# Level scores in two column tiles, four samples' outputs at once, the gate's second product stacked, samples' rows transposed once: one decoder layer on one Trainium2 core

## The chip, the cores and the metric

The kernel runs on one core of a Trainium2 chip. The metric is the device time of one execution in microseconds (us). The core has five engines with queues of their own: PE (TensorE: matrix products, with PEld for the loads of their stationary operand), DVE (VectorE), ACT (ScalarE), POOL (GpSimd) and SP (SyncE, which here only issues DMAs).

## The reference

One inference step of a decoder layer for a new sequence of 512 positions and 8 samples with one new token each; the model's width is 2048. All is float32.

```python
def mixer(xn, ...):
    proj = xn @ w_in
    bg, cg, hin, q, k, v, og, glr = jnp.split(proj, [...])
    cu, conv_new = causal_dwconv(cg * hin, conv_prev, conv_w)
    ya = bg * cu
    logf = jax.nn.log_sigmoid((glr @ gate_w2 + gate_b).astype(f32)) / GATE_TAU
    ...
    o, s_new = gla_chunked(qh, kh, vh, lf, gla_prev.astype(f32), chunk)
    ...
    out = jnp.concatenate([ya, yb], axis=-1) @ w_out
```

```python
def trunk(x, ...):
    m, c_new, s_new = mixer(rmsnorm(x, norm_mix_g[l]), ...)
    x = x + m
    f, f_new = conv_ffn(rmsnorm(x, norm_ffn_g[l]), ...)
    x = x + f
    return rmsnorm(x, final_norm_g), ...
```

The gated linear attention (GLA) has 4 heads with keys of 128 and values of 256 columns. Per position S = diag(a) S + k^T v and o = q S; a comes from the gate, glr @ gate_w2, with a rank of 16. For the new sequence S starts at zero, for each of the 8 samples from its state of 128 x 256 in HBM, and the new states are outputs too. The mixer is followed by an output projection and a feed-forward block of width 5632.

## The kernel before, in words

Activations stand with the model's columns on the partitions and the positions in the free dimension: 512 of the sequence and 8 of the samples make 520 columns, worked on as two halves of 260. Each large product is split into high and low parts (hi, lo) for accuracy: for one block of 128 rows (k) there are three products, hi by hi, hi by lo and lo by hi, for each half of the columns. The weights come as pieces of 128 x 1024 by DMA from SP (raw, L101); ACT makes hi (L111), DVE lo (L112). The products of the mixer's input projection are those of L140, those of the later stages L1247 and L1490.

The start (0 to 55 us): x is loaded with positions on the partitions. For each of the 16 column blocks, x_copy transposes four blocks of 128 x 128 (L378) and the samples' 8 x 128 (L379) into one PSUM bank; ACT (the first four blocks, L383) or DVE (L385) copies all 520 columns to SBUF, POOL sends them to HBM for later (L389), and ACT and DVE split them into hi and lo (L126, L127, and L393, L395 for the first two blocks). The first head's q and k products, twelve a block, run between the transposes. The low rank product glr for all heads (L306) follows, and DVE multiplies its first 32 rows, the products with hi and lo of the weights, by the rows' norm (L532).

The heads (55 to about 420 us): product groups of 16 blocks x 6 products fill PE. After each 4 blocks (24 products), a tick, the generator gla_head puts in one step of a head that is ahead in the data:

- the gate's second product w2s by glr (L879), whose 32 rows hold the rank of 16 twice. ACT and DVE form the log of the gate from it (L883 to L889), and DVE sums it along the positions (L892);
- the diagonal scores of k and q (L930), four products of 128 columns, copied under a mask by DVE into the matrix at (L934);
- seven levels, s = 64, 32, ..., 1. For each, POOL makes differences of the summed gate (e), ACT the exponential (L918), DVE two half-products with q and k into L (L919, L922), and PE multiplies the four chunks of L, 128 columns as weights and the 64 columns of the second halves as data (L982). DVE copies the result under a mask into at (L987). L is made two levels ahead;
- the samples, in four pairs: SP loads a pair's states s0 (L942, three buffers) and v rows vb (L946); ACT scales vb (L952), DVE forms the new state (L955), SP stores it (L959). PE multiplies each by its row of q (L968) into rows 32 j of a PSUM bank, j being the sample's number modulo 4. The state is made at the first four levels, and the product goes behind the third to the sixth level, one pair each;
- transposes of the key matrix (L1033), the samples' selection (L1038), then the outputs (L1053, L1058) and the state of the sequence (L1067, L1071).

In this stage a scheduler with priorities sets the order in which each engine gets these instructions; engines take them in that order, and what cannot start blocks all that is behind it. SP's queue holds the weight pieces, the states' loads and the stores. A weight piece's load waits for DVE to have used the buffer's former content.

A float32 product appears in the profile as two records, one of the split kind (fp32r in a tile's type) as one.

Of the kernel before, what the change touches and what calls it, by code (L numbers as in the profile page):

```python
# [17 lines left out]
P = 128  # L18
D = 2048
KD = D // P  # L20
NP = 512
NS = 8
T = NP + NS
HT = T // 2
NH = 4
DV = 256
# [11 lines left out]
def trunk_kernel(  # L38
# [53 lines left out]
    def tmp():  # L92
        return tp.tile([P, T], F32, tag="t", name="t")
# [37 lines left out]
    def halves(t):  # L131
        return t[:, :HT], t[:, HT:T]
# [52 lines left out]
    idn = cp.tile([P, P], F32, name="idn")  # L185
# [49 lines left out]
    glr = cp.tile([P, T], F32, tag="glr", name="glr")[:32, :]  # L235
    gmix, gffn, gb, gng, cw = (
        par[:, 0:16], par[:, 16:32], par[:, 32:36], par[:, 36:44], par[:, 44:68]
    )
# [20 lines left out]
    masks = {}  # L259
# [23 lines left out]
    with ExitStack() as es:  # L283
# [10 lines left out]
        def low_rank_weights():  # L294
            raw = sp.tile([P, KD, RANK], F32, name="wgraw")
            nc.sync.dma_start(raw, w_in[:, 6144:6160].rearrange("(k p) c -> p k c", p=P))
            nc.scalar.activation(wg[:, :, 0:16], raw, AF.Copy)
# [12 lines left out]

        prow = sp.tile([68, P], F32, name="prow")
        xs = sp.tile([NS, D], F32, name="xs")

        xc = [[sp.tile([P, 4, P], F32, name=f"x0{j}") for j in range(4)]]
        xc += [sp.tile([P, 4, 512], F32, name=f"xc{c}") for c in range(1, 4)]
# [23 lines left out]
        nc.scalar.dma_start(prow[0:16, :], norm_mix_g[0].rearrange("(k p) -> k p", p=P))  # L339
        load_x(xc[0][0], 0)  # L340
        nc.scalar.dma_start(xs, x_sample)
        nc.scalar.preload_act_table_set("natural_log_exp_and_others")
        raws = [load_w(0)]
        for j in (1, 2, 3):
# [30 lines left out]
        def x_copy(k):  # L375
            ps = tps()
            for t in range(4):
                nc.tensor.transpose(ps[:, t * P : (t + 1) * P], x_part(k, t), idn)  # L378
            nc.tensor.transpose(ps[:, NP:T], xs[:, k * P : (k + 1) * P], idn[:NS, :NS])  # L379
            st = tmp()[:, :T]  # L380
            copies[k] = st, ps
            if k < 4:
                nc.scalar.activation(st, ps[:, :T], AF.Copy)  # L383
            else:
                nc.vector.tensor_copy(st, ps[:, :T])  # L385

        def x_split(k):
            st, ps = copies.pop(k)
# [139 lines left out]
        )  # L528
        nc.vector.tensor_copy(R, ps[:, :T])
        low_rank_gate(glr_ps, 8, 8)  # L530
        for o, ps, r in zip(halves(glr), glr_ps, halves(R)):
            nc.vector.tensor_tensor(o, ps[:32, :HT], r[:32, :], op=ALU.mult)  # L532
        state_columns()
        make_masks(sp)
        in_order()
# [3 lines left out]
    def bank():  # L539
        return msp.tile([P, 512], F32, tag="ms", name="ms")  # L540
# [246 lines left out]
    with ExitStack() as mix:  # L787
# [44 lines left out]
        with ExitStack() as gl:  # L832
# [9 lines left out]
            for j in range(4):  # L842
# [4 lines left out]
            w2s = gp.tile([32, 512], F32, name="w2s")  # L847
            for i in range(2):
                nc.sync.dma_start(w2s[16 * i : 16 * (i + 1), :], gate_w2[0])

            done = [0]

# [19 lines left out]
            def gla_head(h, q, k, vt):  # L872
# [3 lines left out]
                for b in range(2):  # L876
                    ps = bank()
                    u = slice(b * HT, (b + 1) * HT)
                    nc.tensor.matmul(  # L879
                        ps[:, :HT], w2s[:, h * P : (h + 1) * P], glr[:, u],  # L880
                        start=True, stop=True,
                    )
# [43 lines left out]

                def scores(lhs, rhs, mask):
                    pb = bank()
                    for c in range(4):
                        nc.tensor.matmul(  # L930
                            pb[:, c * P : (c + 1) * P], lhs[:, c, :], rhs[:, c, :],
                            start=True, stop=True,
                        )
                    nc.vector.copy_predicated(  # L934
                        at, mask[:, None, :].to_broadcast([P, 4, P]),
                        pb.rearrange("p (c i) -> p c i", c=4),
                    )


                def sample_load(b0):  # L940
# [20 lines left out]
                    )  # L961
                    return s0

                def sample_out(b0, s0):
                    for i in range(2):
                        b = b0 + i
                        j = b % 4
                        nc.tensor.matmul(  # L968
                            pos[32 * j : 32 * (j + 1), :DV], qm[:, b, :], s0[:, i, :],
                            start=b < 4, stop=b >= 4, tile_position=(0, 32 * j),  # L970
                        )

                def level_scores(L, s):

                    nb = P // (2 * s)
# [3 lines left out]
                    pb = bank()  # L979
                    rhs = second(L)  # L980
                    for c in range(4):
                        nc.tensor.matmul(  # L982
                            pb[:, c * 64 : (c + 1) * 64], L[:, c, :], rhs[:, c],
                            start=True, stop=True,
                        )
                    mask = masks[s].rearrange("p (n h s) -> p n h s", n=nb, h=2)[:, :, 1, :]
                    nc.vector.copy_predicated(  # L987
                        second(at), mask[:, None].to_broadcast([P, 4, nb, s]),
                        pb[:, :256].rearrange("p (c n s) -> p c n s", c=4, n=nb),
                    )  # L990

                scores(k4, q4, idn8)
                Ls = [level(LEVELS[0])]
# [3 lines left out]
                yield  # L997
                yield
                pos = bank()
                s0 = deque()  # L1000
# [95 lines left out]
            for h in range(NH):  # L1096
# [8 lines left out]
                for o, p, rr in zip(halves(q), ps, halves(R)):  # L1105
                    nc.vector.scalar_tensor_tensor(
                        o, p[:, :HT], QSCALE, rr, op0=ALU.mult, op1=ALU.mult
                    )
                vt = gp.tile([P, 4, DV], F32, tag="vt", name="vt", bufs=2)
                v = []  # L1110
# [173 lines left out]
            if t >= 2:  # L1284
                nc.vector.tensor_tensor(z2, z2, R[:, HT:], op=ALU.mult)

    R2 = cp.tile([P, T], F32, tag="glr", name="R2")
    conv_z = {}

    def mult(out, x, y):  # L1290
# [408 lines left out]
    for i, (kind, at, r) in enumerate(order):  # L1699
# [24 lines left out]
        if j == 0:  # L1724
            if n and groups[n - 1][0] in ("mix", "up"):
                before, (t,) = groups[n - 1]
                steps.append([(gate if before == "up" else mix_gate)(t), i, 0])
            if kind == "wo" and at[0] == 1:
                homes.update(FFN_HOMES)
                if not ssq:  # L1730
                    ssq += [cp.tile([P, T], F32, tag="glr", name="ssq"), R]
# [211 lines left out]
```

## Time and profile before

| | us |
|---|---|
| median of 3 runs | 2163.0 |
| lowest, highest | 2161.82, 2163.73 |
| the profiled execution | 2160.99 |
| its span in the trace | 2159.3 |
| PE busy | 2134.2 |
| DVE busy | 1734.5 |
| ACT busy | 1111.6 |
| POOL busy | 439.7 |

The clock granted to PE was 0.997 of full speed. In a row of the profile stand the line of the kernel, the engine, the operation, the output's and inputs' names (buffer numbers left out: ms is any of the small PSUM banks, mm one of the accumulators, tp a bank of the start), the shapes and the number of instructions. In a timeline the first two numbers are the start and the length of a group of like instructions that follow one another, and the bracket at the end is the idle time before, with what ended it. L numbers are lines of the kernel before.

### The profile page before, as it was taken

What the parts mean: (1) busy time and instruction counts of PE and PEld (TensorE: products, weight loads), DVE (VectorE), ACT (ScalarE), POOL (GpSimd) and SP (SyncE); (2) the same over time, 40 slices, a digit from 0 to 9 for tenths busy, and PEclk for the clock granted to TensorE, in tenths of its full rate; (3) what the DMA queues carried; (4) which work ended last, traced back from release to release, by engine and by line L of the source; (5) the groups of instructions that cost most, each with busy time, mean ns of one, the idle gap of its engine ahead of it and who ended that gap; (6) DMA issues with size and microseconds to landing.
All of it is one profiled execution on the core that took longest, in us unless ns stands there. A gap on an engine that the chain in (4) does not pass through costs nothing.

```text
span 2159.3 us, 43820 instructions
## 1 busy us (share of the span) xinstructions
PE 2134.2 (99%) x17749; PEld 2112.2 (98%) x17749; DVE 1734.5 (80%) x2302; ACT 1111.6 (51%) x1631; POOL 439.7 (20%) x625
## 2 busy tenths in 40 slices
PE   9999999999999999999999999999999999999997
PEld 8999999999999999999999999999999999999997
DVE  7347465588888898998998998998998778888886
ACT  6435435355544586555555555555555554444445
POOL 5113131211243421121221131122121300200000
PEclk9999999999999999999999999999999999999999
DMA  8545464388888996667676676676677866994734
GB/s 258 145 131 157 121 190 121 93 247 215 206 259 248 297 268 181 181 183 189 166 191 176 167 195 179 163 198 178 169 193 192 287 206 161 274 291 134 225 108 158
DMA packets 467163, 415.51 MB, mean 192 GB/s; under 512 B 21641, under 2 KB 426393, under 8 KB 466817
## 3 DMA queue, kind: packets, MB, share of 16 engines
q1 hardware_dynamic: 424081, 289.71, 47.0%
q0 software_dynamic: 42832, 122.93, 21.7%
q8 instruction: 139, 2.28, 0.4%
q14 instruction: 63, 0.52, 0.1%
q10 hardware_dynamic: 48, 0.07, 0.0%
HBM read 299.45 MB, written 80.31 MB: 176 GB/s over the span
## 4 chain that ended last, share of the span: by engine, by line
PE 90%; DMA 3%; DVE 3%; ACT 1%; issue 1%; POOL 0%; SPq 0%; ACTq 0%; DVEq 0%; POOLq 0%
PE mm L1247 34%; PE mm L140 14%; PE ms L1247 14%; PE x L1490 9%; PE y L1490 9%; PE f L1490 3%; PE e L1490 3%; PE ms L982 1%; DMA form<-g_d 1%; DMA g_d<-t 1%; DMA yl<-t_d 0%; DMA yl<-mt_d 0%; PE ms L1836 0%; DMA raw<-raw 0%; PE ms L968 0%
## 5 line engine op out<-in xcount | busy, mean ns | idle before, releaser
L1247 PE MATMUL mm<-yl,hi 128*128 128x260 f32 x1696 | 476.6, 281 | 3.4 <-DVE yl L124 3.4
L1247 PE MATMUL mm<-yh,hi 128*128 128x260 f32 x1696 | 476.1, 281 | 2.4 <-ACT ms L1257 1.2
L1247 PE MATMUL mm<-yh,lo 128*128 128x260 f32 x1696 | 475.2, 280 | 0.8 <-DVE lo L1227 0.8
L1223 ACT ACTIVATE hi<-raw 128x1024 fp32r<-128x1024 f32 x324 | 342.0, 1056 | 233.8 <-issue 89.4
L1227 DVE TENSOR_TENSOR lo<-raw,hi 128x1024 fp32r<-128x1024 f32 x324 | 395.4, 1220 | 36.0 <-ACT hi L1223 33.0
L1227 DVE TENSOR_TENSOR lo<-s,hi 128x1024 fp32r<-128x1024 f32 x243 | 298.4, 1228 | 124.9 <-ACT hi L1223 124.9
L1223 ACT ACTIVATE hi<-s 128x1024 fp32r<-128x1024 f32 x243 | 257.4, 1059 | 220.7 <-PE ms L1247 93.6
L1247 PEld LDWEIGHTS mm<-yl,hi 128*128 128x128 f32 x1696 | 319.8, 189 | 4.0 <-DVE yl L124 4.0
L1247 PEld LDWEIGHTS mm<-yh,hi 128*128 128x128 f32 x1696 | 319.5, 188 | 3.0 <-ACT ms L1257 1.4
L1247 PEld LDWEIGHTS mm<-yh,lo 128*128 128x128 f32 x1696 | 319.2, 188 | 1.2 <-DVE lo L1227 1.2
L1247 PE MATMUL ms<-b,hi 128*128 128x260 f32 x1408 | 266.3, 280 | 0.0
L1247 PEld LDWEIGHTS ms<-b,hi 128*128 128x128 f32 x1408 | 223.2, 189 | 0.0
L1490 PE MATMUL x<-form,hi 128*128 128x260 f32 x1120 | 211.5, 281 | 0.1
L1490 PE MATMUL y<-form,hi 128*128 128x260 f32 x1120 | 211.3, 281 | 0.0
L1168 DVE TENSOR_TENSOR s<-s,raw 128x1024 f32<-128x1024 f32 x162 | 197.9, 1221 | 2.8
L1247 PE MATMUL ms<-b,lo 128*128 128x260 f32 x704 | 198.1, 281 | 0.0
L1490 PEld LDWEIGHTS x<-form,hi 128*128 128x128 f32 x1120 | 176.4, 188 | 0.7 <-issue 0.5
L1490 PEld LDWEIGHTS y<-form,hi 128*128 128x128 f32 x1120 | 176.4, 188 | 0.3
L112 DVE TENSOR_TENSOR lo<-raw,hi 128x1024 fp32r<-128x1024 f32 x76 | 94.9, 1253 | 78.0 <-ACT hi L111 77.9
L1490 PE MATMUL x<-form,lo 128*128 128x260 f32 x560 | 156.7, 280 | 0.1
L1490 PE MATMUL y<-form,lo 128*128 128x260 f32 x560 | 156.7, 280 | 0.0
L1247 PEld LDWEIGHTS ms<-b,lo 128*128 128x128 f32 x704 | 132.4, 188 | 0.0
(382 smaller groups left out, 5066.2 us busy)
## 6 DMA issues: line engine op xcount, KB each, us to landing
raw<-in_w_up_dram SPq DMA_DIRECT2D x176, 512.0 KB, 4.6
raw<-in_w_down_dram SPq DMA_DIRECT2D x96, 512.0 KB, 4.7
raw<-in_w_in_dram SPq DMA_DIRECT2D x92, 512.0 KB, 4.5
form<-f_d SPq DMA_DIRECT2D x126, 260.0 KB, 6.2
raw<-raw POOLq DMA_DIRECT2D x56, 512.0 KB, 5.9
f_d<-t POOLq DMA_DIRECT2D x80, 260.0 KB, 5.6
raw<-in_w_out_dram SPq DMA_DIRECT2D x32, 512.0 KB, 13.8
form<-g_d POOLq DMA_DIRECT2D x42, 260.0 KB, 7.6
```

The costliest lines, as they stand in the source:

```text
L112: nc.vector.tensor_tensor(lo, raw, hi.bitcast(F32), op=ALU.subtract)
L140: nc.tensor.matmul(o, w, xx, start=first and i == 0, stop=last and i == 2)
L982: nc.tensor.matmul(pb[:, c * 64 : (c + 1) * 64], L[:, c, :], rhs[:, c], start=True, stop=True,)
L1168: return lambda: nc.vector.tensor_tensor(out, x, y, op=ALU.add)
L1223: nc.scalar.activation(his[i], src, AF.Copy)
L1227: nc.vector.tensor_tensor(los[i], src, his[i].bitcast(F32), op=ALU.subtract)
L1247: nc.tensor.matmul(st["bank"][b], w[:, k, :], x, start=b not in st["used"] and k == 0 and j == 0, stop=k == 7 and j == 2, skip_group_check ...
L1490: nc.tensor.matmul(ps[:, m, :], w[:, k, m * P : (m + 1) * P], x, start=b not in st["used"] and k == 0 and j == 0, stop=k == 3 and j == 2, ...
```

## The change

Four parts of the heads and of the start are computed in another arrangement.

1. Levels and diagonal scores. The 128 weight columns of a chunk are cut into two tiles of 64, at columns 0 and 64 of PE. A level's product takes from each half only the data columns that belong to it (32 instead of 64), so there are eight products where there were four, and two masked copies on DVE, each over 64 partitions, where there was one. The widest level, s = 64, needs one tile and a plain copy. (L953, L1002, L1017; the copies L958, L1006, L1024.)
2. Samples' outputs. Four samples' products go together, behind the third level (samples 0 to 3) and the fifth (4 to 7), each on its own tile of 32 columns (L990).
3. The gate's second product. glr and w2s get 96 rows: high by high, high by low and low by high in one stacked product of the split kind (L900). For that ACT makes three copies of the gate's weights at the start and POOL two; glr is copied by ACT, and multiplied and split in head 0 by DVE and ACT; w2s is loaded six times and split.
4. Samples' rows of x. For 14 of the 16 column blocks the transpose of 8 rows (L379 before) goes; one transpose of 128 x 128 of the samples' rows, laid out anew by a DMA, takes their place, and POOL puts each block's 8 columns beside the sequence's 512, which ACT and DVE copy alone.

The scheduler's order changes with it. PE in head 1 before, at the sixth level (its L is L_2441); s0_2406 is the states of pair 3, mm the accumulators of the product group:

```order
L140 MATMUL mm_2461<-bl_97,hi_2465 128x260
L140 MATMUL mm_2462<-cl_99,hi_2465 128x260
L982 MATMUL ms_2547<-L_2441 128x64 [waits DVE_49,PE_49]
L982 MATMUL ms_2547<-L_2441 128x64 x3
L968 MATMUL ms_2293<-s0_2406,qm_848 32x256 [waits DMAHW7_49,DVE_49]
L968 MATMUL ms_2293<-s0_2406,qm_848 32x256 [waits DVE_49]
L140 MATMUL mm_2461<-xh_100,hi_2471 128x260 [waits Activation_49]
```

The same pair in PE's order now; its state is s0_2478, and s0_2423 is pair 2:

```order
L140 MATMUL mm_2536<-bl_89,hi_2540 128x260
L140 MATMUL mm_2537<-cl_91,hi_2540 128x260
L1017 MATMUL ms_2574<-L_2463 64x32 [waits DVE_49,PE_49]
L1017 MATMUL ms_2574<-L_2463 64x32 x7
L990 MATMUL ms_2353<-s0_2423,qm_858 32x256 [waits DMAHW2_49]
L990 MATMUL ms_2353<-s0_2423,qm_858 32x256
L990 MATMUL ms_2353<-s0_2478,qm_858 32x256 [waits DMAHW4_49,DVE_49]
L990 MATMUL ms_2353<-s0_2478,qm_858 32x256 [waits DVE_49]
L140 MATMUL mm_2536<-bh_92,hi_2540 128x260
```

Pair 3's products have moved from behind the sixth level to behind the fifth, into one step with pair 2's.

SP in head 1 before, around the load of pair 3's states (s0_2406); raw are weight pieces, s0_3144 is a load for the next head:

```order
L946 DMA vb_2408<-v_d_123 128x512 [waits DMAHW3_49]
L101 DMA raw_2638<-in_w_in_dram 128x8x128 [waits DMAHW4_49,DVE_49]
L959 DMA out_6_dram<-s0_2358 128x2x256 [waits DMAHW5_49,DVE_49]
L101 DMA raw_2784<-in_w_in_dram 128x8x128 [waits DMAHW6_49,DVE_49]
L942 DMA s0_2406<-in_state_gla_dram 128x2x256 [waits DMAHW7_49,DMAHW0_49,PE_49]
L942 DMA s0_3144<-in_state_gla_dram 128x2x256 [waits DMAHW2_49,PE_49]
```

And now, with pair 3's states in s0_2478:

```order
L970 DMA vb_2480<-v_d_123 128x512 [waits DMAHW0_49]
L101 DMA raw_2728<-in_w_in_dram 128x8x128 [waits DMAHW1_49,DVE_49]
L101 DMA raw_2874<-in_w_in_dram 128x8x128 [waits DMAHW3_49,DMAHW2_49,DVE_49]
L983 DMA out_6_dram<-s0_2423 128x2x256 [waits DVE_49]
L966 DMA s0_2478<-in_state_gla_dram 128x2x256 [waits DMAHW5_49,DMAHW4_49,PE_49]
L966 DMA s0_3239<-in_state_gla_dram 128x2x256 [waits DMAHW6_49,PE_49]
```

The load of pair 3's states still stands behind two weight pieces; the store of pair 2's states has moved behind the second piece.

The diff, cut to its core:

```diff
+            for i in range(3):
+                nc.scalar.activation(wg[:, :, 32 * i : 32 * i + 16], raw, AF.Copy)
...
+            for i in (1, 2):
+                nc.gpsimd.tensor_copy(
+                    wg[:, :, 32 * i + 16 : 32 * i + 32], wg[:, :, 16:32].bitcast(F32)
+                )
...
-            nc.tensor.transpose(ps[:, NP:T], xs[:, k * P : (k + 1) * P], idn[:NS, :NS])
+            if k < 2:
+                nc.tensor.transpose(ps[:, NP:T], xs[:, k * P : (k + 1) * P], idn[:NS, :NS])
...
+            if k == 2:
+                nc.tensor.transpose(ps[:, NP : NP + P], xsr, idn)
+                nc.vector.tensor_copy(xsT.rearrange("p k b -> p (k b)"), ps[:, NP : NP + P])
+            if k >= 2:
+                nc.gpsimd.tensor_copy(st[:, NP:], xsT[:, k, :])
...
-                        ps[:, :HT], w2s[:, h * P : (h + 1) * P], glr[:, u],
+                        ps[:, :HT], w2s[:, h * P : (h + 1) * P], glr[:96, u],
...
-                def sample_out(b0, s0):
-                    for i in range(2):
-                        b = b0 + i
-                        j = b % 4
+                def sample_out(b0):
+                    for j in range(4):
                         nc.tensor.matmul(
-                            pos[32 * j : 32 * (j + 1), :DV], qm[:, b, :], s0[:, i, :],
-                            start=b < 4, stop=b >= 4, tile_position=(0, 32 * j),
+                            pos[32 * j : 32 * (j + 1), :DV], qm[:, b0 + j, :],
+                            s0[j // 2][:, j % 2, :],
+                            start=b0 == 0, stop=b0 == 4, tile_position=(0, 32 * j),
                         )
...
-                        nc.tensor.matmul(
-                            pb[:, c * 64 : (c + 1) * 64], L[:, c, :], rhs[:, c],
-                            start=True, stop=True,
+                        for t in tiles:
+                            nc.tensor.matmul(
+                                pb[t, c * 32 : (c + 1) * 32], L[:, c, t],
+                                second(L[:, c : c + 1, t])[:, 0],
+                                start=True, stop=True, tile_position=(0, t.start),
+                            )
+                    for t in tiles:
...
+                    if i in (2, 4):
+                        sample_out(2 * i - 4)
                     if i < 4:
                         s0.append(sample_pair(2 * i, *loaded))
-                    if 2 <= i < 6:
-                        sample_out(2 * i - 4, s0.popleft())
...
+                if h == 0:
+                    nc.vector.tensor_tensor(gate_rows, gate_rows, R[:96, :], op=ALU.mult)
+                    nc.scalar.activation(glr[:96, :], gate_rows, AF.Copy)
+                    nc.vector.tensor_tensor(
+                        glr[64:96, :], gate_rows[64:96, :], glr[64:96, :].bitcast(F32),
+                        op=ALU.subtract,
+                    )
```

More of the change, by code (lines that the diff above doesn't have):

```diff
@@ L234, in trunk_kernel @@
     R = cp.tile([P, T], F32, name="R")
-    glr = cp.tile([P, T], F32, tag="glr", name="glr")[:32, :]
+    glr = cp.tile([P, T + 3], F32R, tag="glr", name="glr")[:, 3:]
     gmix, gffn, gb, gng, cw = (
@@ L378, in x_copy @@
                 nc.tensor.transpose(ps[:, t * P : (t + 1) * P], x_part(k, t), idn)
-            nc.tensor.transpose(ps[:, NP:T], xs[:, k * P : (k + 1) * P], idn[:NS, :NS])
+            n = T if k < 2 else NP
+            if k < 2:
+                nc.tensor.transpose(ps[:, NP:T], xs[:, k * P : (k + 1) * P], idn[:NS, :NS])
             st = tmp()[:, :T]
             copies[k] = st, ps
+            if k == 2:
[3 more added lines that the diff above has]
+                nc.gpsimd.tensor_copy(st[:, NP:], xsT[:, k, :])
             if k < 4:
-                nc.scalar.activation(st, ps[:, :T], AF.Copy)
+                nc.scalar.activation(st[:, :n], ps[:, :n], AF.Copy)
             else:
-                nc.vector.tensor_copy(st, ps[:, :T])
+                nc.vector.tensor_copy(st[:, :n], ps[:, :n])
         def x_split(k):
@@ L530, in trunk_kernel @@
         low_rank_gate(glr_ps, 8, 8)
-        for o, ps, r in zip(halves(glr), glr_ps, halves(R)):
-            nc.vector.tensor_tensor(o, ps[:32, :HT], r[:32, :], op=ALU.mult)
+        gate_rows = tmp()[:96, :T]
+        for o, ps in zip(halves(gate_rows), glr_ps):
+            nc.scalar.activation(o, ps[:96, :HT], AF.Copy)
         state_columns()
@@ L846, in trunk_kernel @@
                 )
-            w2s = gp.tile([32, 512], F32, name="w2s")
-            for i in range(2):
-                nc.sync.dma_start(w2s[16 * i : 16 * (i + 1), :], gate_w2[0])
+            w2raw = wp.tile([P, 1024], F32, tag="raw", name="raw")[:96, :512]
+            for i in range(6):
+                nc.sync.dma_start(w2raw[16 * i : 16 * (i + 1), :], gate_w2[0])
+            w2s = gp.tile([96, 512], F32R, name="w2s")
+            nc.scalar.activation(w2s, w2raw, AF.Copy)
+            nc.vector.tensor_tensor(
+                w2s[32:64, :], w2raw[32:64, :], w2s[32:64, :].bitcast(F32), op=ALU.subtract
+            )
             done = [0]
@@ L928, in scores @@
                     pb = bank()
+                    tiles = [slice(t, t + 64) for t in (0, 64)]
                     for c in range(4):
-                        nc.tensor.matmul(
-                            pb[:, c * P : (c + 1) * P], lhs[:, c, :], rhs[:, c, :],
-                            start=True, stop=True,
-                        )
[L934 to L937, printed above, removed]
+                        for t in tiles:
+                            nc.tensor.matmul(
+                                pb[t, c * 64 : (c + 1) * 64], lhs[:, c, t], rhs[:, c, t],
+                                start=True, stop=True, tile_position=(0, t.start),
+                            )
+                    for t in tiles:
+                        nc.vector.copy_predicated(
+                            at[t, :, t], mask[t, None, t].to_broadcast([64, 4, 64]),
+                            pb[t, :256].rearrange("p (c i) -> p c i", c=4),
+                        )
                 def sample_load(b0):
@@ L962, in sample_pair @@
                     return s0
-                def sample_out(b0, s0):
-                    for i in range(2):
-                        b = b0 + i
-                        j = b % 4
+                def sample_out(b0):
+                    for j in range(4):
                         nc.tensor.matmul(
-                            pos[32 * j : 32 * (j + 1), :DV], qm[:, b, :], s0[:, i, :],
-                            start=b < 4, stop=b >= 4, tile_position=(0, 32 * j),
+                            pos[32 * j : 32 * (j + 1), :DV], qm[:, b0 + j, :],
+                            s0[j // 2][:, j % 2, :],
+                            start=b0 == 0, stop=b0 == 4, tile_position=(0, 32 * j),
                         )
+                    s0.clear()
                 def level_scores(L, s):
-                    nb = P // (2 * s)
+                    pb = bank()
+                    if s == 64:
+                        for c in range(4):
+                            nc.tensor.matmul(
+                                pb[:64, c * 64 : (c + 1) * 64], L[:, c, :64], L[:, c, 64:],
+                                start=True, stop=True,
+                            )
+                        nc.vector.tensor_copy(
+                            at[:64, :, 64:], pb[:64, :256].rearrange("p (c i) -> p c i", c=4)
+                        )
+                        return
+                    nb = 32 // s
                     second = lambda x: x.rearrange(
@@ L978, in level_scores @@
                     )[:, :, :, 1, :]
-                    pb = bank()
-                    rhs = second(L)
+                    tiles = [slice(t, t + 64) for t in (0, 64)]
                     for c in range(4):
-                        nc.tensor.matmul(
-                            pb[:, c * 64 : (c + 1) * 64], L[:, c, :], rhs[:, c],
-                            start=True, stop=True,
-                        )
[L986 to L990, printed above, removed]
+                        for t in tiles:
+                            nc.tensor.matmul(
+                                pb[t, c * 32 : (c + 1) * 32], L[:, c, t],
+                                second(L[:, c : c + 1, t])[:, 0],
+                                start=True, stop=True, tile_position=(0, t.start),
+                            )
+                    for t in tiles:
+                        mask = masks[s][t, t].rearrange("p (n h s) -> p n h s", n=nb, h=2)
+                        nc.vector.copy_predicated(
+                            second(at[t, :, t]),
+                            mask[:, None, :, 1, :].to_broadcast([64, 4, nb, s]),
+                            pb[t, :128].rearrange("p (c n s) -> p c n s", c=4, n=nb),
+                        )
                 scores(k4, q4, idn8)
@@ L1285, in up_finish @@
                 nc.vector.tensor_tensor(z2, z2, R[:, HT:], op=ALU.mult)
-    R2 = cp.tile([P, T], F32, tag="glr", name="R2")
+    R2 = cp.tile([P, T + 3], F32, tag="glr", name="R2")[:, 3:]
     conv_z = {}
@@ L1730, in trunk_kernel @@
                 if not ssq:
-                    ssq += [cp.tile([P, T], F32, tag="glr", name="ssq"), R]
+                    ssq += [cp.tile([P, T + 3], F32, tag="glr", name="ssq")[:, 3:], R]
                 steps.append([projected(at[1]), i, 0])
```

8 lines of the change are left out of this document (6 added, 2 removed).

## The prediction

> **What bounds the kernel now.** I read the page's busy shares first, then the table of windows over the stages that the change touches, then PE's timeline there.
>
> ```profile
> span 2159.3 us, 43820 instructions
> ...
> PE 2134.2 (99%) x17749; PEld 2112.2 (98%) x17749; DVE 1734.5 (80%) x2302; ACT 1111.6 (51%) x1631; POOL 439.7 (20%) x625
> ```
> ```profile
> 12.80:22.00 9.20, 9.19 (x70) 8.16 (x69) 6.23 (x12) 5.20 (x11) 2.17 (x4) 1.00 1.09 366
> 22.00:31.00 9.00, 9.00 (x71) 8.25 (x70) 7.10 (x13) 7.28 (x18) 3.22 (x5) 1.00 0.98 328
> 31.00:42.00 11.00, 10.39 (x80) 9.44 (x79) 10.93 (x12) 7.81 (x14) 6.40 (x9) 1.00 0.89 246
> ...
> 170.00:255.00 85.00, 83.16 (x672) 79.44 (x671) 52.47 (x88) 36.23 (x57) 19.21 (x24) 1.00 0.46 137
> ```
>
> PE is busy in all but 25 us of the span. Behind each stretch and its length stand the busy times of PE, PEld, DVE, ACT and POOL. Work taken off PE moves the end, but only where nothing else is nearly as late. Two places are in doubt: DVE at the start (10.93 of 11.00 us in the third row), and the attention heads, where PE already idles for 1.84 us in head 1 (the last row). The profiled execution took 2160.99 us, 2.0 under the median of 2163.0; the sum is made against the former and the difference carried to the latter.
>
> **The change part by part: what it takes off PE.** First the levels, in PE's timeline of head 0.
>
> ```profile
> 101.38 0.40 PE L140 MATMUL mm<-xl,hi 128*128 128x260 f32 x2
> 101.62 1.00 PE L982 MATMUL ms<-L 128*128 128x64 f32 x8
> 102.42 0.48 PE L140 MATMUL mm<-xh,hi 128*128 128x260 f32 x2
> 102.74 0.40 PE L140 MATMUL mm<-xh,lo 128*128 128x260 f32 x2
> ```
>
> Two products of 260 columns take 0.24 us (101.38 to 101.62). The level holds PE for 0.80, and the pair behind it takes 0.32 instead of 0.24: 0.88 in all. Its eight records follow every 0.10 us though each streams a quarter of the columns of a product that needs 0.12, so what paces them is the 128-column weight load of each. After the change there are 16 records, in eight pairs on the two halves of the columns, each with a load of 64 columns. Whether the halves work at the same time is shown by the samples' outputs, which already lie on column tiles, of 32 (PE, then PEld).
>
> ```profile
> 109.14 1.00 PE L982 MATMUL ms<-L 128*128 128x64 f32 x8
> 110.07 0.63 PE L968 MATMUL ms<-s,qm 128*32 128x256 f32 x4
> 110.62 0.39 PE L140 MATMUL mm<-bh,hi 128*128 128x260 f32 x1
> 110.85 0.28 PE L140 MATMUL mm<-ch,hi 128*128 128x260 f32 x1
> ```
> ```profile
> 110.06 0.14 PEld L968 LDWEIGHTS ms<-s,qm 128*32 128x32 f32 x4
> ```
>
> Four records of 0.39 us each fill only 0.63, and four loads only 0.14: the two tiles run side by side, in two steps that start 0.24 apart. Level and pair take 1.48 up to the next product, which is late by another 0.11 (0.23 instead of 0.12): 1.59, of it 0.71 for the pair, 0.48 for its two steps and 0.23 for going into the tiles and out again. So a level in two tiles takes 8 steps of 0.05 (a load half as wide) to 0.10 (no faster) and 0.23: 0.63 to 1.03. I take 0.74, near the low end because the 32-column loads were short. 24 levels (all but the widest, 4 heads) give 24 x 0.14 = 3.4 us (from -3.6 to +6); the diagonal scores and the widest level, with as many loads, 8 x 0.13 = 1.0. [...]
>
> Four samples at once are again two steps, 0.48 and part of the 0.23, since PE comes from column tiles already: 0.6 instead of 1.42, 8 x 0.82 = 6.6 us (1.8 if the four tiles take turns in pairs). Next the gate's second product.
>
> ```profile
> 88.09 1.14 PE L879 MATMUL ms<-glr,w2s 32*128 32x260 f32 x4
> 89.16 0.50 PE L140 MATMUL mm<-xh,hi 128*128 128x260 f32 x2
> 89.50 0.40 PE L140 MATMUL mm<-xh,lo 128*128 128x260 f32 x2
> ```
>
> It takes 1.07, the pair behind it is late by 0.10, and it started 0.09 late: 1.26. Two products of 260 columns of the ordinary kind take its place: 0.24. Four heads save 4.1 us. GLA in all: 3.4 + 1.0 + 6.6 + 4.1 = 15.1.
>
> At the start, four transposes and the samples' small one stand against four plain ones, whose price is shown by those of v in head 0:
>
> ```profile
> 31.64 0.60 PE L378 MATMUL tp<-idn,xc 128*128 128x128 f32 x4
> 32.33 0.50 PE L140 MATMUL mm<-xh,hi 128*128 128x260 f32 x2
> 32.67 0.40 PE L140 MATMUL mm<-xh,lo 128*128 128x260 f32 x2
> ```
> ```profile
> 69.70 0.60 PE L856 MATMUL ms<-idn,v 128*128 128x128 f32 x4
> 70.06 0.36 PE L140 MATMUL mm<-bh,hi 128*128 128x260 f32 x1
> 70.27 0.28 PE L140 MATMUL mm<-ch,hi 128*128 128x260 f32 x1
> ```
>
> 0.69 + 0.10 against 0.36 + 0.09: the small one costs 0.34. Fourteen go, one of 128 columns comes (0.1): 4.7 us. The whole sum for PE is 19.8 us.
>
> **What takes it back.** Pair 3, samples 6 and 7, is the large item. Its product stood behind the sixth level; now it goes with pair 2 behind the fifth (s = 4), one tick of 24 products earlier. PE's rows give where the outputs behind the fifth level start in the four heads, DVE's where the pair's two updated states (L955) are made; SP's show the load that they wait for.
>
> ```profile
> 118.99 0.63 PE L968 MATMUL ms<-s,qm 128*32 128x256 f32 x4
> ...
> 202.53 0.63 PE L968 MATMUL ms<-s,qm 128*32 128x256 f32 x4
> ...
> 286.22 0.63 PE L968 MATMUL ms<-s,qm 128*32 128x256 f32 x4
> ...
> 385.92 0.63 PE L968 MATMUL ms<-s,qm 128*32 128x256 f32 x4
> ```
> ```profile
> 118.10 0.88 DVE L955 SCALAR_TENSOR_TENSOR s<-s,asm,vb 128x256 f32<-128x256 f32 x2 [3.67 <-issue]
> ...
> 205.12 1.95 DVE L955 SCALAR_TENSOR_TENSOR s<-s,asm,vb 128x256 f32<-128x256 f32 x2 [1.95 <-DMA s<-in_state_gla_dram]
> ...
> 287.94 0.48 DVE L955 SCALAR_TENSOR_TENSOR s<-s,asm,vb 128x256 f32<-128x256 f32 x1
> ...
> 386.43 0.51 DVE L955 SCALAR_TENSOR_TENSOR s<-s,asm,vb 128x256 f32<-128x256 f32 x1
> ```
> ```profile
> 200.25 0.37 SPq L101 DMA_DIRECT2D raw<-in_w_in_dram  x1
> 200.72 1.03 SPq L942 DMA_DIRECT2D s<-in_state_gla_dram  x2
> ```
>
> The states are ready at 118.98, 207.07, 288.42 and 386.94. PE would come to these outputs earlier by 1.02 (gate) + 0.13 + 0.13 (scores, widest level) + 4 x 0.14 (four levels) + 0.82 (first four samples) = 2.66 us. Were the states no earlier, PE would wait 2.65, 7.20, 4.86 and 3.68: 18.4 us, more than the 15.1 saved. They will be somewhat earlier: the load stands in SP's queue behind a weight piece that waits for DVE, whose work follows a chain that the gate's product starts. The gate and the scores give that chain 1.15 us; if it all went with PE it would gain 2.66 and no wait would be new. I take 1.4, near the low end, as the wait is for a DMA (4.4 us from 200.72 to 205.12) and for queues that PE does not drive: 5.6 us in four heads. Queued behind the waiting product are PE's own products, so the wait is paid in full.
>
> The levels' own inputs also bind:
>
> ```profile
> PE ms L982 <- DVE L L922: 1.3, 3, 0.7
> ```
> ```profile
> 200.14 0.44 DVE L987 COPY_PREDICATED at<-mask,ms 128x256 f32<-128x256 uint8 x1
> ```
>
> Three levels find PE waiting already, two of them in head 1, where the gate's saving of 1.0 us will mostly turn into more of it; and each level adds a second masked copy on DVE (two of half the width for the one of 0.44, 0.0 to 0.4 more each). I take 1.3 for head 1 and 0.4 for each other head, 2.5 us (0 to 5). PE held there is not held at pair 3 again: its wait is 18.4 - 5.6 - 2.5 = 10.3. GLA keeps 15.1 - 2.5 - 10.3 = 2.3 us; with a chain gain of 1.15 it keeps 1.3, with 2.66 it keeps 7.
>
> At the start DVE is idle for 2.97 + 1.90 + 0.07 = 4.9 us in the three windows, so 4.7 us less on PE would use it up entirely. POOL gets fourteen small copies and two copies of the gate's weights, and DVE pays while POOL works:
>
> ```profile
> 34.35 2.44 DVE L112 TENSOR_TENSOR lo<-raw,hi 128x1024 fp32r<-128x1024 f32 x1
> ```
> ```profile
> L112 DVE TENSOR_TENSOR lo<-raw,hi 128x1024 fp32r<-128x1024 f32 x76 | 94.9, 1253 | 78.0 <-ACT hi L111 77.9
> ```
>
> Busy time and the mean in ns are the two numbers behind the bar: 2.44 us here against 1.25 as a rule. Each column block's split now also waits for POOL's copy, with the next products behind it. I take half, 2.5 us (1 to 4.7). Two more copies on ACT, the input rows' extra load, and in head 0 a multiply, a copy and two subtractions lie in stretches where ACT or DVE is idle for over a quarter of the time; that idle time covers them (some 3 us of engine time without it).
>
> Sum: 2.3 + 2.5 = 4.8 us saved, 2156.2 for the profiled execution, 2158 against the median. By the terms' ends it lies between 2151 (7 + 4.7) and 2161 (1.3 + 1).
>
> **The rivals.** (a) Nothing takes it back: pair 3 moves with PE, DVE keeps up at the start. 19.8 us saved, 2143. For it speaks that all of PE's sums are from rows; against it the DMA wait at 205.12.
>
> (b) The column tiles' loads do not overlap anything, so the tiled levels and scores pay 16 steps: 0.8 to 1.6, so 1.2. Levels lose 24 x 0.32 = 7.7 instead of gaining 3.4, scores lose about 1.3. But PE then comes to pair 3 later by some 2.3 us a head, and most of that wait goes, as does part of the wait for levels. In GLA 15.1 - 11.1 - 1.8 = 2.2 is left, less 1.1 and some 1.4 of waits, with 2.5 at the start: about 2161, no difference that can be told.
>
> (c) Slower: pair 3's states land late. A load of the same queue in head 1 has taken far longer than 4.4 us:
>
> ```profile
> 187.84 0.47 SPq L946 DMA_DIRECT2D vb<-v_d  x1
> ```
> ```profile
> 194.98 0.51 ACT L952 ACTIVATE vb<-vb,k 128x256 f32<-128x256 f32 x1 [2.17 <-DMA vb<-v_d]
> ```
>
> That is 7.1 us. If PE runs ahead and the weights' loads crowd the state's load to that, each head waits 2.7 us more: +11, so 2169. From 1.2 us later a head (landing after 5.6 us) the gain is gone.
>
> **How the numbers follow.** This kernel's measurement can tell about 0.2%, 4.3 us, from no change: faster means under 2158.7, slower over 2167.3. The forecast has 0.55, of it 0.40 faster, 0.13 same, 0.02 slower, since its centre lies at the edge and the chain's gain was taken low. (a) has 0.10, all faster. (b) has 0.12: 0.03, 0.08, 0.01. (c) has 0.18: 0.03 same, 0.15 slower. 0.05 is for what I do not see, shared by same and slower (0.03, 0.02). Together: faster 0.53, same 0.27, slower 0.20. The range leaves out most of (a) and the far end of (c): 2145 to 2168.
>
> **What would show it.** Right: L990 behind the fifth level waits for DVE's state update or its load in each head, by 1.5 to 4 us; levels near 0.74; gate 0.24; k blocks of the start under 2.0 us apart but with DVE full. Wrong: levels over 0.9 (b), no wait at L990 (a), waits over 5 us (c), or PE waiting elsewhere in the heads.

## The result and the profile after

The changed kernel's median is 2164.67 us against 2162.3 us before (22 runs each; one of the changed kernel's took 7107.61 us and is left out of the ratio); the ratio is 1.0014, with a 95% interval of 1.0007 to 1.002. It is slower by 2.4 us, less than the 0.2% that was to count, but on the other side of the forecast of 2158. The profiled execution took 2167.36 us, 2.7 more than the median, so single sums of its trace are some us too large; before's took 2160.99, 1.3 under its median.

The page and the windows of the heads (PE, PEld, DVE, ACT, POOL busy, then the granted clock):

```profile
PE 2128.5 (98%) x17952; PEld 2104.0 (97%) x17952; DVE 1748.6 (81%) x2332; ACT 1112.7 (51%) x1637; POOL 447.8 (21%) x641
```
```profile
88.00:170.00 82.00, 80.51 (x721) 76.61 (x720) 40.79 (x74) 38.55 (x65) 18.07 (x23) 0.98 0.55 157
170.00:255.00 85.00, 79.48 (x695) 74.72 (x694) 52.65 (x93) 35.56 (x56) 19.66 (x24) 0.96 0.44 127
255.00:355.00 100.00, 96.57 (x866) 92.83 (x866) 60.23 (x105) 46.13 (x76) 26.14 (x32) 1.00 0.55 159
355.00:420.00 65.00, 62.24 (x569) 58.14 (x568) 43.62 (x77) 25.59 (x42) 17.24 (x20) 0.97 0.39 113
```

PE is busy for 5.7 us less than before, and the end is later. In head 1's window it idles for 5.5 us instead of 1.84, and in three of the windows the granted clock falls under 1.00. PE's waits up to 460 us, summed by what ended them, of after:

```profile
PE ms L990 <- DVE s L979: 7.2, 8, 1.8
PE ms L1017 <- DVE L L943: 3.2, 4, 1.4
PE mm L140 <- DVE lo L112: 1.1, 2, 0.6
...
PE ms L1002 <- DVE L L943: 0.9, 1, 0.9
```

L990 are the samples' outputs, L979 the states that they need. The outputs were not among PE's waits before, nor were those for the weights' low parts (L112). The prices of the instructions are nearly those forecast: a level is 16 records in 0.6 us, the four samples follow in 0.57 where two pairs took 1.42, and the gate's product stands in the stream for 0.24.

```profile
108.16 0.66 PE L1017 MATMUL ms<-L 128*64 128x32 f32 x16
108.74 0.64 PE L990 MATMUL ms<-s,qm 128*32 128x256 f32 x8
109.31 0.39 PE L140 MATMUL mm<-bh,hi 128*128 128x260 f32 x1
```
```profile
88.25 0.40 PE L900 MATMUL ms<-glr,w2s 96*128 96x260 f32 x2
88.49 0.41 PE L140 MATMUL mm<-xh,hi 128*128 128x260 f32 x2
```

From a level's start to the next product it takes 1.15 us with four samples' outputs behind it, when nothing is waited for (behind the third level of head 0). The same place behind the fifth level of head 1:

```profile
201.23 0.66 PE L1017 MATMUL ms<-L 128*64 128x32 f32 x16
201.82 0.63 PE L990 MATMUL ms<-s,qm 128*32 128x256 f32 x4
204.26 0.62 PE L990 MATMUL ms<-s,qm 128*32 128x256 f32 x2 [1.82 <-DVE s L979]
205.70 1.06 PE L990 MATMUL ms<-s,qm 128*32 128x256 f32 x2 [0.82 <-DVE s L979]
206.69 0.59 PE L140 MATMUL mm<-bh,hi 128*128 128x260 f32 x1
207.07 0.42 PE L140 MATMUL mm<-ch,hi 128*128 128x260 f32 x1
207.29 0.42 PE L140 MATMUL mm<-bh,lo 128*128 128x260 f32 x1
```

The first pair of outputs runs at once, the two of the other pair come one by one as DVE makes the states, and the next product starts 5.46 us behind the level, 4.3 late. In heads 0, 2 and 3 the same stretch takes 4.15, 3.89 and 4.34: 13.2 us too much in the four. Of these the list above counts the 7.2 in which PE is idle; the rest is the outputs' own time, as they come one by one, and a slow clock in the last of them (1.06 us here instead of 0.62; the clock granted from 205.7 to 206.7 us was 0.50). The last two rows show a second price: products come every 0.22 us instead of 0.12, at a granted clock of 0.50 (206.7 to 211.6 us). That lasts for 5 us here; the 24 products up to the next level take 4.30, 5.30, 3.06 and 4.02 us in the four heads, 4.4 us more than four times head 2's.

### The profile page after: what moved, and what is told of

Same layout as the page of the kernel before. It is cut to its first block, busy times and chain, and to the rows that moved or that the text cites. A ratio compares the mean times of both kernels' runs of the same rounds, so it can differ in the third digit from the quotient of the medians.

```text
span 2165.6 us, 44293 instructions
## 1 busy us (share of the span) xinstructions
PE 2128.5 (98%) x17952; PEld 2104.0 (97%) x17952; DVE 1748.6 (81%) x2332; ACT 1112.7 (51%) x1637; POOL 447.8 (21%) x641
## 4 chain that ended last, share of the span: by engine, by line
PE 85%; DVE 7%; DMA 3%; issue 2%; ACT 2%; POOL 1%; SPq 0%; DVEq 0%; ACTq 0%; POOLq 0%
PE mm L1292 34%; PE ms L1292 14%; PE mm L140 13%; PE x L1535 8%; PE y L1535 8%; PE e L1535 3%; PE f L1535 3%; DVE lo L1272 1%; DMA raw<-in_w_out_dram 1%; DVE lo L112 1%; DVE s L979 1%; DMA yl<-mt_d 1%; DMA x_d<-acc 1%; DVE yl L124 0%; PE ms L1881 0%
## 5 line engine op out<-in xcount | busy, mean ns | idle before, releaser
L1268 ACT ACTIVATE hi<-raw 128x1024 fp32r<-128x1024 f32 x324 | 341.8, 1055 | 233.6 <-issue 88.2
L112 DVE TENSOR_TENSOR lo<-raw,hi 128x1024 fp32r<-128x1024 f32 x76 | 95.6, 1261 | 72.4 <-ACT hi L111 72.2
L111 ACT ACTIVATE hi<-raw 128x1024 fp32r<-128x1024 f32 x76 | 79.6, 1052 | 106.5 <-PE mm L140 100.7
## 6 DMA issues: line engine op xcount, KB each, us to landing
raw<-in_w_out_dram SPq DMA_DIRECT2D x32, 512.0 KB, 10.3
```

The lines of the kernel that those rows point to most:

```text
L111: nc.scalar.activation(hi, raw, AF.Copy)
L112: nc.vector.tensor_tensor(lo, raw, hi.bitcast(F32), op=ALU.subtract)
L1268: nc.scalar.activation(his[i], src, AF.Copy)
```

## The experiments

Theory A: PE waits behind the fifth level for the states of pair 3, and pays a slow clock on top. Rival B: the levels' inputs or DVE's second masked copies are as late, so that moving the outputs would not help. All times are medians, and ratios are against the kernel before.

**The outputs of samples 4 to 7 one level later.**

```diff
-                    if i in (2, 4):
-                        sample_out(2 * i - 4)
+                    if i in (2, 5):
+                        sample_out(4 * (i == 5))
```

> The changed kernel with the outputs of samples 4 to 7 one level later, behind the sixth (s = 2) instead of the fifth. Theory A (PE waits at these outputs for the states of pairs 2 and 3, some 16 us in the four heads of the changed kernel's trace, and the slow clock behind the waits costs another 5): the place is 24 products and a level, 3.65 us, later, so at most 0.9 us of wait a head is left, no slow stretch, and the kernel takes 2145 to 2152 us, 0.6 to 0.9% under the kernel before. Rival B (the levels' inputs, or DVE with its second masked copy, are as late as the states): PE then waits at the sixth or seventh level instead, and the time stays within 5 us of the changed kernel.

Measured: 2150.52 us, ratio 0.9946 (0.9934 to 0.9959), 11.9 us faster than before and, by the medians, 14.2 faster than the changed kernel. The place in head 1, of this kernel:

```profile
200.33 0.66 PE L1017 MATMUL ms<-L 128*64 128x32 f32 x16
200.92 0.64 PE L990 MATMUL ms<-s,qm 128*32 128x256 f32 x8
201.49 0.50 PE L140 MATMUL mm<-xh,hi 128*128 128x260 f32 x2
```

The eight records run together, and the next product follows 1.16 us behind the level. L990 is gone from the list of waits. What is left there, of the heads:

```profile
PE ms L1017 <- DVE L L943: 2.7, 4, 1.4
PE mm L140 <- DVE lo L112: 1.1, 2, 0.6
PE ms L1002 <- DVE L L943: 0.9, 1, 0.9
```

The windows of the heads show the clock at 1.00 again, and 82.11 us of PE in head 1's 85:

```profile
88.00:170.00 82.00, 82.00 (x762) 78.84 (x762) 45.49 (x83) 42.08 (x70) 19.15 (x24) 1.00 0.55 156
170.00:255.00 85.00, 82.11 (x755) 78.59 (x752) 54.18 (x96) 38.93 (x62) 19.38 (x24) 1.00 0.52 152
```

Of theory A the wait holds, and B does not; what the slow clock costs by itself this run does not separate. This version beats both kernels.

**Two levels later.** The same edit with `i in (2, 6)`.

> The changed kernel with the outputs of samples 4 to 7 two levels later, behind the seventh (s = 1). Theory A: no wait for states is left, so it takes as long as the variant behind the sixth level or up to 3 us less. Against it: the states' buffers are held longer, so the next head's loads start later, and ACT's copy of the outputs comes later; if that matters PE waits at the next head's first outputs and the time is above the other variant's.

Measured: 2152.37 us, 0.9956 (0.9943 to 0.9968). No wait for states either, and not faster than behind the sixth level, where the waits were gone already. The medians differ by 1.9 us the other way, within intervals that overlap.

**The wait filled with work.**

```diff
                 def sample_out(b0):
+                    if b0:
+                        fill = bank()
+                        for _ in range(12):
+                            nc.tensor.matmul(fill[:, :P], ones, ones, start=True, stop=True)
```

> The changed kernel with twelve products of ones ahead of the outputs of samples 4 to 7 in each head, some 3.1 us of PE work that nothing needs, put where PE waits anyway. Theory A with the slow clock as a cost of its own: PE never idles for long, the stretches with products every 0.22 us behind the outputs go, and the kernel is 3 to 5 us faster than the changed one although PE does 12 us more work (2160 to 2163). If the slow stretches cost nothing, or come from something else than the idle time: the same as the changed kernel or up to 2 us slower.

Measured: 2165.06 us, 1.001 (1.0001 to 1.0019), as long as the changed kernel. Head 1 of this kernel (L992 are the products of ones, L994 the outputs):

```profile
199.17 0.66 PE L1021 MATMUL ms<-L 128*64 128x32 f32 x16
199.76 2.94 PE L992 MATMUL ms<-ones 128*128 128x128 f32 x24
202.63 0.64 PE L994 MATMUL ms<-s,qm 128*32 128x256 f32 x8
203.20 0.38 PE L140 MATMUL mm<-bh,hi 128*128 128x260 f32 x1
203.42 0.28 PE L140 MATMUL mm<-ch,hi 128*128 128x260 f32 x1
203.54 0.28 PE L140 MATMUL mm<-bh,lo 128*128 128x260 f32 x1
```

As expected the wait and the slow products behind it are gone (a granted clock of 1.00 in all four windows of the heads), and 2.87 us of useless work a head, 11.5 us, fit in their place. The time did not fall by the 3 to 5 us expected; it is what was expected if the slow stretches cost nothing. The trace is less simple. From the first gate product to the end of the heads this profiled execution takes 369.0 us, the changed kernel's 375.1, and that of the version behind the sixth level 357.4. So in the heads the filling gains 6.1 us, and the wait and the slow clock cost 17.7, near 13.2 + 4.4. Behind the heads the filled kernel loses 3.3 us again (185.7 against 184.6 us in the output projection, 1519.8 against 1517.6 behind it), for which no run here shows a cause. By the medians, wait and slow clock are worth 14.2 us in the version behind the sixth level and about these 11.5 here.

The changed kernel's times spread more than those of the filled one, 2160.4 to 2172.3 us against 2162.4 to 2167.3, and its longer runs have the lower clock: 0.998 was granted in the shortest, 0.993 in the longest. The mean is 0.9953 in its 21 runs and 0.9969 in the filled kernel's 11; the difference over 2165 us is 3.5 us, an estimate from these clocks of what the slow clock takes on average. How much of it lies behind the waits, and what the median would be without it, stays open.

**The samples' old arrangement, the rest changed.** sample_out as before, a pair behind each of the third to sixth levels.

> The changed kernel with the old arrangement of the samples' outputs: one pair behind each of the third to sixth levels. PE does 6.8 us more (8 x 0.85). Theory A: pair 3 is due one level later again, so its wait and the slow stretches go, and the kernel takes 2150 to 2156 us, faster than before by 0.3 to 0.6% although a part of the change is undone. Rival B (levels or DVE are as late): it stays at the changed kernel's time or above.

Measured: 2155.48 us, 0.9968 (0.9956 to 0.9981). With a part undone that saves PE 6.8 us it is 9.2 us faster than the changed kernel.

**Pair 2's states in place of pair 3's.**

```diff
-                            s0[j // 2][:, j % 2, :],
+                            s0[0 if b0 else j // 2][:, j % 2, :],
```

> The changed kernel, in which the outputs of samples 6 and 7 are computed from the states of samples 4 and 5 (so they are not the ones asked for); everything else, the place behind the fifth level too, stays, and pair 3's states are still loaded, made and stored. Theory A (the wait is for pair 3 alone): PE waits for pair 2 at most, about 1.8 us in head 1, and the kernel takes 2149 to 2153 us, within 3 us of the variant with the outputs behind the sixth level. Rival (the wait is for pair 2 as well, or for the bank or the four tiles at once): more than 5 us above that variant, 2156 or more.

Measured: 2151.05 us, 0.9946 (0.9934 to 0.9959), the same as with the outputs one level later. The outputs of samples 6 and 7 are not the right ones in this kernel. L990 is not among the waits, not even for pair 2. The wait is for pair 3 alone, not for the bank, the tiles or the place.

**Each part alone, in the kernel before.** Samples:

> The kernel before with the samples' part of the change alone. Theory A: PE saves 8 x 0.83 = 6.7 us, but comes to pair 3's states 0.8 us earlier and one level and 24 products too early; by the rows of the kernel before that is 0.8 + 5.4 + 3.0 + 1.9 = 11 us of waits, with a slow clock behind some of them (0 to 5): 3 to 9 us slower than before, 2165 to 2171. Rival (the samples' part is a gain, and another part of the change brings the loss): 2156 to 2160.

Measured: 2167.89 us, 1.0027 (1.0017 to 1.0038): 5.6 us slower, the only part with a clear loss. In the heads its trace has (L966 are the outputs, L955 the states):

```profile
PE ms L966 <- DVE s L955: 4.9, 4, 2.5
```

Levels and scores:

> The kernel before with levels and diagonal scores in two column tiles alone. The changed kernel's trace has 0.79 for a level against 0.89 and 0.81 for the scores and the widest level against 0.89: 24 x 0.10 + 8 x 0.08 = 3.0 us less for PE. Part of it goes into longer waits for the levels' inputs and the second masked copy on DVE. 1 to 3 us faster than before, 2159.5 to 2161.5. If the second copies on DVE cost more than that they make the kernel slower: over 2163.

Measured: 2158.53 us, 0.9983 (0.9975 to 0.9992): 3.8 us faster, more than the 1 to 3 expected and slightly more than the 3.0 that PE saves, which lies within the interval. The second copies cost nothing that shows here, though waits for the levels' inputs grow to 4.5 us from 1.3.

The gate:

> The kernel before with the stacked gate product alone: 0.24 instead of 1.26 in four heads, 4.1 us less for PE. In head 1 it turns into a longer wait for the levels' input (about 1), and at the end of the start PE waits some 0.4 longer, because DVE multiplies the gate's rows ahead of the first k. 2 to 3 us faster than before, 2159 to 2160.5.

Measured: 2163.27 us, 1.0 (0.9991 to 1.0009): no gain that can be told, where 2 to 3 us were expected. In this kernel's head 1, whose window (170 to 255 us) has a granted clock of 0.98:

```profile
184.46 0.28 PE L140 MATMUL mm<-cl,hi 128*128 128x260 f32 x1
186.49 1.10 PE L993 MATMUL ms<-L 128*128 128x64 f32 x8 [1.75 <-DVE L L933]
...
188.19 0.42 PE L140 MATMUL mm<-bl,hi 128*128 128x260 f32 x1
```

The 1.0 us saved ahead of it has joined the wait for the widest level's input (0.72 before) to one of 1.75, and behind it products come every 0.22 us until 191. That head is 0.8 us longer than before, the other three are 1.0 shorter each. Of these 2.2 us some 0.9 is lost ahead of the heads: the first gate product comes at 91.0 us, against 90.1 in the samples-alone kernel, whose start lacks the gate's part. What takes the rest is not shown.

The start:

> The kernel before with part 4 alone: the samples' rows of x transposed once. PE saves 14 x 0.34 - 0.1 = 4.7 us at the start, but DVE is busy back to back there and POOL's squares of x hold up its two-input operations. Theory A: 0.5 to 2 us faster than before, 2160 to 2162, and in the trace PE waits for DVE's xl. Rival (DVE keeps up): 4 us or more faster, under 2158.5.

Measured: 2161.2 us, 0.9991 (0.9982 to 0.9999): 0.9 us faster, not 4.7. PE waits twice for xl, 1.1 us (once, 0.6, before).

**Parts undone in the version with the outputs behind the sixth level.** Part 4 undone:

> The variant with the outputs behind the sixth level, with part 4 undone: the samples' rows transposed block by block as before. It shows what part 4 is worth beside the others. Theory A (DVE sets the pace of the start): 0.5 to 2 us slower than the variant, 2151 to 2152.5. Rival (the whole saving of 4.7 arrives): 2155.

Measured: 2154.01 us, 0.9957 (0.9944 to 0.9969). Between the two expected: 3.5 us more than the version by the medians, 2.4 by the ratios; the two were measured on different chips, and their intervals overlap. The gate's part undone:

> The variant with the outputs behind the sixth level, with the gate's part undone: 1.26 us for the gate's product in each head again, without the copies of its weights at the start and the extra multiply in head 0. Alone the gate's part gained nothing that could be told. If its saving of 4.1 us is lost to longer waits for the levels' inputs here too: within 1 us of the variant, 2149.5 to 2151.5. If it is worth its 1.0 us in every head but head 1, less some 1 us at the start: 1.5 to 2.5 us slower than the variant, 2152 to 2153.

Measured: 2154.41 us, 0.9962 (0.9948 to 0.9976), 3.9 us more by the medians, 3.5 by the ratios. That is more than the 1.5 to 2.5 expected, but the intervals overlap. It points to a worth of the gate's part once nothing else holds PE up, though alone it showed none; it is not shown.

**POOL's squares earlier.** The four squares of x in the blocks 4 to 7 instead of 8 to 11.

> The variant with the outputs behind the sixth level, with POOL's four squares of x (1.05 us each) issued between the column blocks 4 to 7 instead of 8 to 11, when DVE still has idle time. In the variant's trace DVE's xl takes 1.67 us beside them instead of 0.75, twice, and PE waits 1.7 us for xl. Theory A (POOL's squares slow DVE on the path of the start): the wait of 1.7 goes and the kernel is 1 to 2.5 us faster than the variant, 2148 to 2149.5. Rival (DVE has no idle time early either, or POOL's small copies do it): within 1 us of the variant, 2150 to 2152.

Measured: 2152.56 us, 0.9954 (0.994 to 0.9967): no faster, as the rival has it, and a little above its 2150 to 2152. PE's wait for xl falls from 1.7 to 0.8 us, and 1.3 us of waits for bl and cl come in. DVE's two-input operations are now long here, beside the squares (DVE, then POOL):

```profile
23.14 0.47 DVE L127 SCALAR_TENSOR_TENSOR cl<-t,gm,ch 128x260 fp32r<-128x260 f32 x1
23.54 0.68 DVE L400 COPY t<-tp 128x512 f32<-128x512 f32 x1
24.14 2.03 DVE L127 SCALAR_TENSOR_TENSOR bl<-t,gm,bh 128x260 fp32r<-128x260 f32 x1
26.10 1.26 DVE L127 SCALAR_TENSOR_TENSOR cl<-t,gm,ch 128x260 fp32r<-128x260 f32 x1
```
```profile
24.17 1.05 POOL L507 TENSOR_TENSOR x<-x 128x512 f32<-128x512 f32 x1
...
25.88 1.19 POOL L507 TENSOR_TENSOR x<-x 128x512 f32<-128x512 f32 x1
```

## Why the prediction was wrong, point by point

- **What PE gains** was right. A level came out at 0.79 us (taken: 0.74), four samples at 0.57 (0.6), the gate at 0.24 (0.24): 24 x 0.10, 8 x 0.08, 8 x 0.85 and 4.1 give 13.9 us where the forecast had 15.1. The second rival, tiles that do not run side by side (1.2 us a level), is out.
- **The wait for pair 3** was named, with its place, and taken as 10.3 us. In the profiled execution it is 13.2, by the delay of the next product. The step that failed is "I take 1.4": the states were to come 1.4 us earlier in each head, because the gate's product starts their chain. Counted from the gate's product they were ready after 30.9, 37.1, 33.5 and 32.4 us before (88.1, 170.0, 254.9 and 354.5 to the ends of L955), and after 31.0, 34.8, 33.1 and 32.6 now (from 88.2, 170.9, 259.7 and 360.2): 2.3 us earlier in head 1 alone, and 2.3 in all instead of 5.6. That is 0.6 a head, less than the 1.15 taken as the least. The load itself did move. In head 0 it was issued at 113.92 before, and now:

```profile
112.45 1.04 SPq L966 DMA_DIRECT2D s<-in_state_gla_dram  x2
```

  Counted from the gate's product it was issued after 25.8, 30.7, 27.1 and 26.4 us before, and after 24.2, 28.2, 26.4 and 25.9 now: some 5.2 us earlier in all, near the 5.6. But from its issue to the second of the pair's states it took 5.1, 6.3, 6.4 and 6.1 us before and takes 6.8, 6.5, 6.7 and 6.7 now, some 2.9 more. DVE in head 0, where the two states followed each other before (118.10):

```profile
116.96 0.48 DVE L979 SCALAR_TENSOR_TENSOR s<-s,asm,vb 128x256 f32<-128x256 f32 x1 [3.56 <-DMA s<-in_state_gla_dram]
117.48 0.62 DVE L1024 COPY_PREDICATED at<-mask,ms 64x128 f32<-64x128 uint8 x2
...
118.80 0.48 DVE L979 SCALAR_TENSOR_TENSOR s<-s,asm,vb 128x256 f32<-128x256 f32 x1
```

  DVE idles for 3.56 us until the load lands, and then puts 1.3 us of the levels' work between the two states. In head 1 DVE is idle too, for 1.54 us, until 4.6 us behind the load's issue. In heads 2 and 3 it isn't. Head 2:

```profile
288.98 0.41 DVE L943 TENSOR_TENSOR L<-e,k 128x256 f32<-128x256 f32 x1
289.43 0.63 DVE L1024 COPY_PREDICATED at<-mask,ms 64x128 f32<-64x128 uint8 x2
290.09 0.43 DVE L940 TENSOR_TENSOR L<-e,q 128x256 f32<-128x256 f32 x1
290.43 0.83 DVE L943 TENSOR_TENSOR L<-e,k 128x256 f32<-128x256 f32 x1
291.19 1.65 DVE L979 SCALAR_TENSOR_TENSOR s<-s,asm,vb 128x256 f32<-128x256 f32 x2
```

  The first row makes the input of the fifth level, which PE starts at 289.55; the last row makes pair 3's states. Between them DVE works without a gap on the previous level's two copies and the next level's input, 1.8 us, so PE, which needs 0.6 us from the level to the outputs, meets the states 1.5 and 2.7 us later whatever it saved before. In this head the load (issued at 286.15) was not the last to come, and the prediction looked only at the load.
- **"The wait is paid in full"** was too little. Behind three of the four waits products ran at nearly half their pace, 4.4 us in the profiled execution, a term that the sum did not have. The clock granted in these stretches (120.2 to 122.9, 206.7 to 211.6 and 393.9 to 395.9 us) was 0.50, against 1.00 behind head 2's wait (293.4 to 296.4), and the pace 0.217 against 0.119 us a product. How long a wait it takes is not shown: one of 1.75 us was enough in the kernel with the gate alone, and in head 3 waits of 0.95 and 0.56 behind 0.71 were, while the same two in head 2, behind 1.40, brought none.
- **The levels' inputs** were sized rightly: 3.2 + 0.9 against 1.3 us, 2.8 more (taken: 2.5). Waits of 1.1 us for the weights' low parts were not in the forecast. The sum for the heads, 13.9 - 2.8 - 1.1 - 13.2 - 4.4 = -7.6, is near what the two traces give: from the first gate product to the first product behind the heads 367.8 us before and 375.1 now.
- **The start** was forecast at 2.5 us (1 to 4.7); alone it gained 0.9. The reason held: DVE is full there (11.00 of the 11.00 us from 31 to 42 in that kernel), and in the version behind the sixth level its xl takes 1.67 us beside POOL's squares and 0.75 elsewhere. Undoing part 4 in that version cost 2.4 to 3.5, with intervals that overlap.
- **The rivals.** The second's 2161 lies nearest to the median, but its tiles are refuted. The third has the right sign by another mechanism: its loads did not land much later (from issue to the first state 4.5 us in head 0 and 4.6 in head 1, against 4.2 and 4.4 before). The sign was missed because the terms that failed, 2.9 us more of wait for pair 3 and 4.4 us of slow products, are together larger than the 4.8 that was left as the forecast.

## What to carry to other kernels

Before a result is asked for earlier, read the queue of the engine that makes it from the last thing that engine made for the same consumer: what stands between the two is a wait that moves along with the consumer and can't be won back by making the consumer faster. In heads 2 and 3 it was that queue that set the time, in heads 0 and 1 a load, with DVE's queue behind it in head 0. Here one level's delay, two numbers in the code, turned a loss of 2.4 us into a gain of 11.9. A wait of PE in the middle of the stream cost more than its length here, so the slow products behind it (0 to 2.2 us a head in the profiled execution, at a granted clock of 0.50) belong in the sum as a term of their own.

## What the runs showed of the hardware that was not expected

The pace of PE at the start differs from execution to execution. The 14 records of products of ones at 6 us take 1.83 us in the kernel before and 3.35 in the changed one's profiled execution. Where they take 3.35, the first of the ordinary products comes at 12.77 us (the changed kernel), 12.71 (the gate alone) and 12.80 (samples alone, 3.36 there), against 10.78 in the kernel before. The clock granted from 5 to 8 us is given as 1.00 both before and in the changed kernel, so it is not shown what slows them. With the start as it was before, the first gate product then comes at 90.1 us (samples alone) instead of 88.1 and 88.3 (before, levels alone); with the changed start it comes at 88.2 instead of 87.3 to 87.6, though at 88.8 in one trace where they are short (the samples' old arrangement, with a granted clock of 0.97 from 0 to 55 us). So two profiled executions may differ by up to 2 us before the first head. The gate-alone kernel's times fall into two groups, 2160.6 to 2161.5 and 2163.3 to 2164.7; that this comes from the start is not shown.

```profile
6.29 3.35 PE L368 MATMUL mm<-ones 128*128 128x128 f32 x14
```

DVE's two-input operations were slow beside POOL's two-input squares: 0.47 us became 2.03 and 1.26 beside two of them. In the kernel before, the split that took 2.44 us instead of 1.25, from 34.35, stands beside one square:

```profile
34.65 1.06 POOL L492 TENSOR_TENSOR x<-x 128x512 f32<-128x512 f32 x1
```

The rows do not show what makes the one slow beside the other. Moving the squares, tried in one other place, did not make the kernel faster.
